# Sparse attention in a two-block transformer: values by pairs of heads in alternating column halves, biases from one reversed row per head

## The chip, the core and the metric

The kernel runs on one core of one Trainium2 chip. Its engines work side by side, each through its own instructions in order: TensorE (PE) multiplies matrices, ScalarE (ACT) and VectorE (DVE) compute on elements, GpSimd (POOL) does a few powers here and issues transfers of its own (the software queue), and SyncE (SP) issues the other transfers (DMA). On-chip memory is SBUF, with 128 partitions, and PSUM, into which PE writes. The metric is the device time of one execution in microseconds (us), as the median of several.

## What is computed

Two blocks of two layers each work on 256 tokens of width 1024 in float32. A layer of block 1 has a large input projection, a retention, a sparse attention (NSA) and a feed-forward part. The change is in the sparse attention, with its 16 heads of 64 columns in 2 groups:

```
def head_bias(dist):
    return jnp.moveaxis(table[t5_bucket(dist)], (-2, -1), (0, 1))
...
lc = jnp.einsum('bghqd,bgnd->bghqn', qx, kc) * scale + head_bias(dc)
pc = masked_softmax(lc, dc >= 0)
oc = jnp.einsum('bghqn,bgnd->bghqd', pc.astype(vc.dtype), vc)
...
ls = jnp.einsum('bghqd,bgqkld->bghqkl', qx, ksel) * scale + sel_bias(ds)
os_ = jnp.einsum('bghqm,bgqmd->bghqd', ps.astype(vsel.dtype), ...)
...
lw = jnp.einsum('bghqd,bgld->bghql', qx, kw) * scale + head_bias(dw)
ow = jnp.einsum('bghql,bgld->bghqd', pw.astype(vw.dtype), vw)
return gx[..., 0:1] * oc + gx[..., 1:2] * os_ + gx[..., 2:3] * ow
```

With 256 tokens every block of keys is selected and the window holds all earlier tokens, so the selected and the window branch both are causal attention over all 256 tokens, with different keys and values. The bias depends on the head and on the distance of query and key alone. The compressed branch has 15 keys.

## The kernel before

PE's foreground is the projections: an item per 512 KB of weights, in a fixed order. SP loads the weights into `raw` (5 buffers; those of the compression into `u`), ACT copies them rounded to `whi`, DVE forms the rest `wlo`, and PE multiplies with both. Everything else (heads of the attention, retention, the set-up of the biases, the end of the compression) is written as generators that run beside the items. A planner at build time (class `Beside`) counts the work of each engine, advances a generator when its step is due by that count and PE has room, and so sets the order on each engine. `use` books an instruction's cost, `arrives` says when a loaded tile is expected, `PACE` (9 us) spaces some steps of the bias set-up. At run time every engine keeps this order and waits on semaphores.

`make_bias` runs once, in layer 1. Two products with a one-hot table give each head's bias by distance: `rb` (16 rows of 384, in DRAM) and `rc` (640 x 16). From `rc` POOL gathers `z<-rc` (L728), and a product with a flip matrix makes `biasc`, the bias of the compressed keys. From `rb` the step `spread` (L711) loads two heads' rows into all 128 partitions (L713, 384 KB) and writes them to `bd`, 128 copies of each head's row in DRAM (L715, 384 KB); eight such pairs cover the 16 heads. A head may start when its rows are there ("bias ready") and the compression has ended (`flags`).

`nsa_head` is one head; four make a quad, two quads share a group. It loads its bias from `bd` with a row step of 383 elements (L873; 4 buffers), so that each partition is shifted by one. PE forms the scores from `KH`, `KL` and the queries; DVE adds the bias and takes the row maxima in one instruction (`add_max`, L203); ACT takes the exponential; the result is scaled and transposed on PE into `PT` (a `z` tile, 6 buffers). Then come the values: four matmuls of `vnat` and `PT` into `O`, a PSUM bank of the quad. Their stationary operand has 64 columns, so a head fills one half of PE's columns: even heads write partitions 0 to 63, odd ones 64 to 127. A matmul of float32 appears in the trace as two records, and each of the trace's weight loads goes with one. After head 3 the quad's compressed part (`vblk`) is added.

Two groups of matmuls of block 2 have the same shape: `b<-z,V` (L1542) does, in one step, a 256 and a 128 wide matmul in one half of the columns and then the same in the other; `b<-w,V` (L1586) does one head, so one half, per step.

Of the kernel before, what the change touches and what calls it, by code (L numbers as in the profile page):

```python
# [10 lines left out]
F32 = mybir.dt.float32  # L11
# [84 lines left out]
SLACK_ROPE, SLACK_STICK, SLACK_DIFF, SLACK_DSA = 2.0, 2.0, 3.0, 2.0  # L96
PUMP_PE = 0.8
BACKLOG = 6.0
PACE = 9.0


@with_exitstack
def tile_kernel(ctx: ExitStack, tc: tile.TileContext, A: dict, out: bass.AP):
    nc = tc.nc
# [8 lines left out]
    dr = ctx.enter_context(tc.tile_pool(name="scratch", bufs=1, space=bass.MemoryType.DRAM))  # L113
# [4 lines left out]
    def zt(shape, dt=F32):  # L118
        return up.tile(shape, dt, name="z", tag="z", bufs=NB_Z)

    def w2(shape, dt=F32):
        return up.tile(shape, dt, name="w", tag="w", bufs=NB_W)
# [4 lines left out]
    def bank(shape):  # L127
        return ps.tile(shape, F32, name="b", tag="b", bufs=8)
# [3 lines left out]
    eng = {"P": 0.0, "A": 0.0, "V": 0.0, "G": 0.0, "D": 0.0}  # L132
    done_at, step, tables, filler = {}, [0.0], [None], [False]
    TABLES = {AF.Exp: 0, AF.Tanh: 0, AF.Gelu_apprx_tanh: 1, AF.Silu: 2, AF.Ln: 3, AF.Sin: 4}

    def key(o):
        return o.tensor.name

    def use(e, ns, outs, ins):
        at = max([done_at.get(key(i), 0.0) for i in ins if hasattr(i, "tensor")] + [0.0])  # L140
        cost = ns / 1e3
        if filler[0]:

            eng[e] += cost
            t = max(eng[e], at + cost)
        else:
            t = eng[e] = max(eng[e], at) + cost
        for o in outs:
            if o is not None:
                done_at[key(o)] = t + 0.1  # L150
        step[0] = max(step[0], t + 0.1)
# [5 lines left out]
    def arrives(t, us):  # L157

        done_at[key(t)] = eng["P"] + us
        step[0] = max(step[0], eng["P"] + us)  # L160

    def width(o):
        n = 1
        for z in o.shape[1:]:
            n *= z
        return n
# [12 lines left out]
    def vec(outs, ins, n=None):  # L179
        use("V", (n or width(outs[0])) / 0.96 + 70, outs, ins)  # L180
# [16 lines left out]
    def copy_v(o, i):  # L197
        nc.vector.tensor_copy(o, i)
        vec([o], [i])
# [12 lines left out]
        nc.vector.reciprocal(o, i)  # L212
        vec([o], [i], 8 * width(o))

    def mm(o, lhsT, rhs, start, stop):
        nc.tensor.matmul(o, lhsT, rhs, start=start, stop=stop, skip_group_check=True)  # L216
        n = width(rhs)
        if rhs.dtype == F32R:
            ns = n / 2.4 * (1 if n >= 256 else 4)
        else:  # L220
            ns = n / 0.6 * width(lhsT) / 128
        use("P", ns, [o], [lhsT, rhs])


    cts = {}
# [5 lines left out]
    def C(name):  # L231
        g, o, n = CW[name]
        return cts[g][:, o:o + n]
# [8 lines left out]
    def warm_up(n):  # L242

        z, b = w2([128, 512]), bank([128, 512])
        nc.vector.memset(z, 0.0)
        for _ in range(n):
            mm(b[:, :256], z[:, :128], z[:, :256], True, True)
# [15 lines left out]
    def split(src, hi, lo, scale=1.0):  # L263
        copy_a(hi, src, scale)
        lo_of(lo, src, hi, scale)
# [174 lines left out]
    S = {}  # L440

    def proj_T(w2d, c0, ncols, x, nkt, evac, r0=0, runs=1, stride=0, pre=None):


        cw = 256 // runs
        for ci, c in enumerate(range(0, ncols, cw)):
            box = {}
            for k0 in range(0, nkt, 4):
                nk = min(4, nkt - k0)

                def fn(pc, ci=ci, k0=k0, nk=nk, box=box):
                    if pre is not None:
                        pre(k0)
                    if k0 == 0:
                        box["b"] = bank([128, 2, 256])
                    hi, lo = pc
                    xx = S[x]
                    for k in range(nk):
                        kk = k0 + k
                        for ct in range(2):  # L460
                            cs = slice(128 * ct, 128 * ct + 128)
                            wh, wl = hi[:, k, cs], lo[:, k, cs]
                            o = box["b"][:, ct, :]
                            mm(o, wh, xx.H(kk), kk == 0 and ct == 0, False)
                            mm(o, wh, xx.L(kk), False, False)
                            mm(o, wl, xx.H(kk), False, kk == nkt - 1)
                    if k0 + nk == nkt:
                        evac(ci, box["b"])

                items.append(Item(fn, spec(w2d, r0 + 128 * k0, nk, c0 + c, cw, runs, stride)))  # L470
# [219 lines left out]
    def make_bias():  # L690
        bp = S["bp"]
        cz = zt([128, 784])
        tab, oneh = cz[:33, 640:656], cz[:33, :640]
        cts[3] = cz[:, 656:784]
        nc.vector.memset(tab, NEG)
        nc.sync.dma_start(tab[:32], A["rel_bias"])
        nc.sync.dma_start(oneh, A["onehot"])
        nc.sync.dma_start(cts[3], A["const_3"])
        flip = C("flip")
        arrives(cz, 6.0)  # L700
        yield
        b = bank([16, 384])
        mm(b, tab, oneh[:, :384], True, True)
        bs = w2([16, 384])
        copy_v(bs, b)

        rb = dr.tile([16, 384], F32, name="rb")
        nc.sync.dma_start(rb, bs)
        S["bd"] = dr.tile([16, 128, 384], F32, name="bd")

        def spread(j):  # L711
            row = zt([128, 2, 384])
            nc.gpsimd.dma_start(row, bass.AP(tensor=rb.tensor, offset=rb.offset + 384 * j,  # L713
                                             ap=[[0, 128], [384, 2], [1, 384]]))
            nc.gpsimd.dma_start(S["bd"][j:j + 2].rearrange("h p k -> p h k"), row)  # L715

        b = bank([128, 5, 16])
        for j in range(5):
            mm(b[:, j, :], oneh[:, 128 * j:128 * j + 128], tab, j == 0, j == 4)
        bs = w2([128, 5, 16])  # L720
        copy_v(bs, b)
        rc = dr.tile([640, 16], F32, name="rc")
        nc.gpsimd.dma_start(rc.rearrange("(j p) h -> p j h", p=128), bs)
        spread(0)

        rv = zt([128, 2, 16, 16])
        for t in range(2):
            nc.gpsimd.dma_start(rv[:, t], bass.AP(tensor=rc.tensor, offset=rc.offset + (159 - 128 * t) * 16,  # L728
                                                  ap=[[16, 128], [256, 16], [1, 16]]))
        spread(2)  # L730
        arrives(rv, 12.0)
        yield
        b = bank([128, 2, 16, 16])
        mm(b, flip, rv, True, True)
        copy_v(S["biasc"], b)
        for j in range(4, 16, 2):
            spread(j)
            S["bias ready"] = j
            step[0] = eng["P"] + PACE
            yield  # L740
        S["bias ready"] = 16

    def block1_layer(i):
        w = A["w_in"][i]
        kvf, flags = {}, set()
# [119 lines left out]

        def nsa_head(qd, hh):
            g, h, Q = qd // 2, 4 * qd + hh, QD[qd]
            while len(flags) < 2 or S.get("bias ready", 0) <= h:
                yield True
            KH, KL, gates, vnat, vblk, biasc = S["KH"], S["KL"], R["gates"], R["vnat"], R["vblk"], S["biasc"]  # L870
            bias = S["bp"].tile([128, 256], F32, name="bias", bufs=4)
            bd = S["bd"]
            nc.gpsimd.dma_start(bias, bass.AP(tensor=bd.tensor, offset=bd.offset + 49152 * h + 127,  # L873
                                              ap=[[383, 128], [1, 256]]))
            arrives(bias, 3.0)
            yield
            Z = zt([128, 800])
# [49 lines left out]
            PT = zt([128, 768])  # L927
            b = bank([128, 2, 2, 128])
# [8 lines left out]
            yield  # L937
            while Q["pv"] != hh:
                yield True
            if hh == 0:  # L940
                Q["O"] = bank([128, 2, 256])
            O = Q["O"]
            e, c = hh % 2, hh // 2
            o = slice(64 * e, 64 * e + 64)
            for br in range(2):
                vs = slice(128 * br + 64 * g, 128 * br + 64 * g + 64)
                mm(O[o, c, :], vnat[:, 0, vs], PT[:, 256 * br:256 * br + 256], c == 0 and br == 0, False)
                mm(O[o, c, 128:], vnat[:, 1, vs], PT[:, 512 + 128 * br:640 + 128 * br], False, False)
            Q["pv"] += 1
            if hh < 3:  # L950
                return
            b = bank([64, 2, 128])
# [5 lines left out]
            for c in range(2):  # L958
                mm(O[:, c, :], vblk[g][:, 2 * c:2 * c + 2, :].rearrange("p a d -> p (a d)"), PcT, False, c == 1)
            k0 = 2 * qd  # L960
            onT = S["onT"]
            split(O, onT.hi[k0 // 4][:, k0 % 4:k0 % 4 + 2, :], onT.lo[k0 // 4][:, k0 % 4:k0 % 4 + 2, :])
            kept["quad", qd] = True
# [38 lines left out]
        def retention(h):  # L1002
# [27 lines left out]
            for n in range(2):  # L1030
                O = bank([128, 512])
                ms = [(0, 128 * n)] + ([(1, 256)] if n else [])
# [816 lines left out]
```

## Time and profile before

| | |
|---|---|
| median of 3 runs | 2214.05 us (2213.95 to 2215.66) |
| the profiled execution | 2216.03 us |
| its span | 2214.3 us |
| PE busy | 2167.8 us, 98% |
| DVE busy | 1486.1 us, 67% |
| ACT busy | 1236.4 us, 56% |
| read from and written to HBM | 376.60 and 4.26 MB |

The span runs from the first to the last instruction of the program; the rest of an execution's time lies around it. Busy is the union of an engine's instructions. Records of PE overlap, and their ends are modelled, so the distance from one start to the next tells more than a duration. PEclk is the share of its clock that PE was granted.

### The profile page before, as it was taken

The numbers are of one execution on the slowest core, as the hardware profiler recorded it, in microseconds if no ns is written. First come the engines' busy times: TensorE is split into PE (matmuls) and PEld (weight loads), VectorE is DVE, ScalarE is ACT, GpSimd is POOL, SyncE is SP. The second block draws the span as 40 slices with busy tenths as digits, with TensorE's granted clock in tenths as the row PEclk, the third lists the DMA queues.
The fourth block names the chain that finished last, engine by engine and source line by source line (L and its number), as shares of the span: only waits on it lengthen the run. The fifth ranks groups of instructions, "written<-read, shape, count | busy, mean of one in ns | idle before, by whom it ended". The sixth has DMA issues, their size and how long they took to land.

```text
span 2214.3 us, 37531 instructions
## 1 busy us (share of the span) xinstructions
PE 2167.8 (98%) x14692; PEld 1973.1 (89%) x14692; DVE 1486.1 (67%) x2773; ACT 1236.4 (56%) x2044; POOL 115.0 (5%) x131
## 2 busy tenths in 40 slices
PE   8899999999999999999999999999999999989998
PEld 7688899899988888998998999988997999988997
DVE  5677765755576777666555887876557888776555
ACT  4466655544455566554444777655445777555443
POOL 2100100000000000000000010100000000100000
PEclk9999999999999999999999999999999999999999
DMA  9854455565676544555655545455655545455553
GB/s 299 281 150 132 141 153 156 176 199 187 194 223 178 150 139 141 146 180 179 185 187 169 175 134 172 139 174 179 190 188 171 165 144 173 147 163 180 190 186 109
DMA packets 299950, 383.31 MB, mean 173 GB/s; under 512 B 16635, under 2 KB 238987, under 8 KB 299772
## 3 DMA queue, kind: packets, MB, share of 16 engines
q1 hardware_dynamic: 296572, 370.12, 54.2%
q0 software_dynamic: 3200, 10.79, 1.5%
q8 instruction: 115, 1.88, 0.3%
q14 instruction: 63, 0.52, 0.1%
HBM read 376.60 MB, written 4.26 MB: 172 GB/s over the span
## 4 chain that ended last, share of the span: by engine, by line
PE 83%; DVE 9%; ACT 3%; DMA 2%; issue 2%; POOL 1%; SPq 0%; POOLq 0%; DVEq 0%; ACTq 0%
PE b L216 80%; DVE wlo L183 3%; PE b L250 3%; DMA raw<-w_in 2%; DVE u L183 2%; ACT z L169 1%; DVE w L183 1%; POOL s L239 1%; ACT u L169 1%; ACT whi L169 1%; DVE z L194 1%; DVE w L194 0%; DVE z L183 0%; ACT L169 0%; DMA w<-a_lambda 0%
## 5 line engine op out<-in xcount | busy, mean ns | idle before, releaser
L183 DVE TENSOR_TENSOR wlo<-raw,whi 128x1024 fp32r<-128x1024 f32 (+1 forms) x670 | 814.7, 1220 | 449.1 <-ACT whi L169 446.8
L169 ACT ACTIVATE whi<-raw 128x1024 fp32r<-128x1024 f32 (+1 forms) x670 | 704.2, 1056 | 656.8 <-PE b L216 464.7
L216 PE MATMUL b<-u,whi 128*128 128x256 f32 x5760 | 1052.8, 285 | 0.0
L216 PEld LDWEIGHTS b<-u,whi 128*128 128x128 f32 x5760 | 902.6, 192 | 10.0 <-issue 5.3
L216 PE MATMUL b<-u,wlo 128*128 128x256 f32 x2880 | 815.9, 283 | 0.0
L216 PE MATMUL b<-whi,u 128*128 128x512 f32 (+2 forms) x2752 | 811.6, 372 | 1.8 <-ACT whi L169 1.6
L216 PEld LDWEIGHTS b<-whi,u 128*128 128x128 f32 x2752 | 502.0, 189 | 90.9 <-issue 4.9
L216 PEld LDWEIGHTS b<-u,wlo 128*128 128x128 f32 x2880 | 552.7, 192 | 0.0
L216 PE MATMUL b<-wlo,u 128*128 128x512 f32 (+2 forms) x1376 | 509.5, 370 | 0.5 <-DVE wlo L183 0.5
L216 PEld LDWEIGHTS b<-wlo,u 128*128 128x128 f32 x1376 | 260.6, 189 | 39.6 <-DVE wlo L183 1.2
L169 ACT ACTIVATE u<-b 64x512 fp32r<-64x512 f32 (+3 forms) x234 | 133.0, 579 | 101.1 <-PE b L250 52.8
L239 POOL TENSOR_TENSOR s<-s,mhalf 128x1 f32<-128x1 f32 (+3 forms) x60 | 77.5, 1292 | 1508.2 <-DVE s L194 1047.1
L169 ACT ACTIVATE z<-z,s 128x256 f32<-128x256 f32 (+2 forms) x304 | 124.5, 425 | 51.6 <-DVE s L203 39.3
L183 DVE TENSOR_TENSOR u<-b,u 128x512 fp32r<-128x512 f32 (+2 forms) x150 | 98.3, 665 | 21.0 <-ACT u L169 16.8
L169 ACT ACTIVATE w<-b 128x512 f32<-128x512 f32 (+3 forms) x150 | 81.1, 547 | 43.2 <-PE b L216 42.0
L250 PE MATMUL b<-const,w 128*128 128x128 f32 (+1 forms) x416 | 65.3, 280 | 19.5 <-DVE w L194 9.3
L250 PEld LDWEIGHTS b<-const,w 128*128 128x128 f32 (+1 forms) x416 | 47.8, 141 | 31.5 <-issue 13.5
L216 PE MATMUL b<-u 128*128 128x256 f32 (+1 forms) x288 | 42.6, 293 | 14.8 <-ACT u L169 8.6
L169 ACT ACTIVATE u<-w 128x512 fp32r<-128x512 f32 x80 | 49.6, 619 | 11.5 <-DVE w L183 11.5
L216 PEld LDWEIGHTS b<-u 128*128 128x128 f32 x288 | 38.2, 196 | 18.5 <-ACT u L169 9.4
L183 DVE TENSOR_TENSOR w<-w 128x512 f32<-128x512 f32 (+3 forms) x94 | 51.9, 566 | 4.0 <-ACT w L169 3.7
L216 PE MATMUL b<-z,vnat 128*64 128x128 f32 (+1 forms) x256 | 46.8, 332 | 0.0
(145 smaller groups left out, 1233.2 us busy)
## 6 DMA issues: line engine op xcount, KB each, us to landing
raw<-w_in SPq DMA_DIRECT2D x268, 512.0 KB, 3.9
raw<-w_ffn_in SPq DMA_DIRECT2D x80, 512.0 KB, 3.6
raw<-w_up SPq DMA_DIRECT2D x64, 512.0 KB, 3.7
raw<-w_down SPq DMA_DIRECT2D x64, 512.0 KB, 3.5
raw<-w_ffn_out SPq DMA_DIRECT2D x44, 512.0 KB, 3.7
raw<-w_o_ret SPq DMA_DIRECT2D x32, 512.0 KB, 3.4
raw<-w_out SPq DMA_DIRECT2D x32, 512.0 KB, 3.8
raw<-w_o_nsa SPq DMA_DIRECT2D x16, 512.0 KB, 3.4
```

Of the source, the lines that this page charges most:

```text
L169: nc.scalar.activation(o, i, func, bias=bias, scale=scale, accum_out=accum_out)
L183: nc.vector.tensor_tensor(out=out, in0=in0, in1=in1, op=op)
L194: nc.vector.scalar_tensor_tensor(out=out, in0=in0, scalar=scalar, in1=in1, op0=op0, op1=op1)
L216: nc.tensor.matmul(o, lhsT, rhs, start=start, stop=stop, skip_group_check=True)
L239: nc.gpsimd.tensor_tensor(o, i, mhalf[:, :n], op=OP.pow)
L250: nc.tensor.transpose(o, i, C("ident")[:i.shape[0], :i.shape[0]])
```

## The change

A head's values are no longer multiplied when it is done: an even head keeps its `PT` and ends, and the odd head that follows does the matmuls of both, eight in a row that go to the two halves of the columns in turn. `mm` has a new argument `share`, by which the planner books each at half its cost. The copies `bd`, and with them `spread` and `PACE`, go. `rb` now holds each row backwards (the copy out of PSUM reads it in reverse), and a head loads its bias from `rb` itself with a row step of one; `add_max` reads the tile backwards. All heads may start once `biasc` is made. The planner expects the gather from `rc` 16 us after its issue, not 12.

```diff
--- before.py
+++ after.py
@@ -96,7 +96,6 @@
 SLACK_ROPE, SLACK_STICK, SLACK_DIFF, SLACK_DSA = 2.0, 2.0, 3.0, 2.0
 PUMP_PE = 0.8
 BACKLOG = 6.0
-PACE = 9.0
 
 
 @with_exitstack
@@ -212,14 +211,14 @@
         nc.vector.reciprocal(o, i)
         vec([o], [i], 8 * width(o))
 
-    def mm(o, lhsT, rhs, start, stop):
+    def mm(o, lhsT, rhs, start, stop, share=1.0):
         nc.tensor.matmul(o, lhsT, rhs, start=start, stop=stop, skip_group_check=True)
         n = width(rhs)
         if rhs.dtype == F32R:
             ns = n / 2.4 * (1 if n >= 256 else 4)
         else:
             ns = n / 0.6 * width(lhsT) / 128
-        use("P", ns, [o], [lhsT, rhs])
+        use("P", ns * share, [o], [lhsT, rhs])
 
 
     cts = {}
@@ -701,19 +700,11 @@
         yield
         b = bank([16, 384])
         mm(b, tab, oneh[:, :384], True, True)
+
         bs = w2([16, 384])
-        copy_v(bs, b)
-
-        rb = dr.tile([16, 384], F32, name="rb")
+        copy_v(bs, b[:, ::-1])
+        rb = S["rb"] = dr.tile([16, 384], F32, name="rb")
         nc.sync.dma_start(rb, bs)
-        S["bd"] = dr.tile([16, 128, 384], F32, name="bd")
-
-        def spread(j):
-            row = zt([128, 2, 384])
-            nc.gpsimd.dma_start(row, bass.AP(tensor=rb.tensor, offset=rb.offset + 384 * j,
-                                             ap=[[0, 128], [384, 2], [1, 384]]))
-            nc.gpsimd.dma_start(S["bd"][j:j + 2].rearrange("h p k -> p h k"), row)
-
         b = bank([128, 5, 16])
         for j in range(5):
             mm(b[:, j, :], oneh[:, 128 * j:128 * j + 128], tab, j == 0, j == 4)
@@ -721,24 +712,17 @@
         copy_v(bs, b)
         rc = dr.tile([640, 16], F32, name="rc")
         nc.gpsimd.dma_start(rc.rearrange("(j p) h -> p j h", p=128), bs)
-        spread(0)
 
         rv = zt([128, 2, 16, 16])
         for t in range(2):
             nc.gpsimd.dma_start(rv[:, t], bass.AP(tensor=rc.tensor, offset=rc.offset + (159 - 128 * t) * 16,
                                                   ap=[[16, 128], [256, 16], [1, 16]]))
-        spread(2)
-        arrives(rv, 12.0)
+        arrives(rv, 16.0)
         yield
         b = bank([128, 2, 16, 16])
         mm(b, flip, rv, True, True)
         copy_v(S["biasc"], b)
-        for j in range(4, 16, 2):
-            spread(j)
-            S["bias ready"] = j
-            step[0] = eng["P"] + PACE
-            yield
-        S["bias ready"] = 16
+        S["bias ready"] = True
 
     def block1_layer(i):
         w = A["w_in"][i]
@@ -865,13 +849,14 @@
 
         def nsa_head(qd, hh):
             g, h, Q = qd // 2, 4 * qd + hh, QD[qd]
-            while len(flags) < 2 or S.get("bias ready", 0) <= h:
+            while len(flags) < 2 or "bias ready" not in S:
                 yield True
             KH, KL, gates, vnat, vblk, biasc = S["KH"], S["KL"], R["gates"], R["vnat"], R["vblk"], S["biasc"]
             bias = S["bp"].tile([128, 256], F32, name="bias", bufs=4)
-            bd = S["bd"]
-            nc.gpsimd.dma_start(bias, bass.AP(tensor=bd.tensor, offset=bd.offset + 49152 * h + 127,
-                                              ap=[[383, 128], [1, 256]]))
+            rb = S["rb"]
+            nc.gpsimd.dma_start(bias, bass.AP(tensor=rb.tensor, offset=rb.offset + 384 * h + 1,
+                                              ap=[[1, 128], [1, 256]]))
+            bias = bias[:, ::-1]
             arrives(bias, 3.0)
             yield
             Z = zt([128, 800])
@@ -937,16 +922,21 @@
             yield
             while Q["pv"] != hh:
                 yield True
-            if hh == 0:
+            Q["pv"] += 1
+            if hh % 2 == 0:
+                Q["PT"] = PT
+                return
+
+            if hh == 1:
                 Q["O"] = bank([128, 2, 256])
-            O = Q["O"]
-            e, c = hh % 2, hh // 2
-            o = slice(64 * e, 64 * e + 64)
+            O, c = Q["O"], hh // 2
+            pair = [(slice(0, 64), Q.pop("PT")), (slice(64, 128), PT)]
             for br in range(2):
                 vs = slice(128 * br + 64 * g, 128 * br + 64 * g + 64)
-                mm(O[o, c, :], vnat[:, 0, vs], PT[:, 256 * br:256 * br + 256], c == 0 and br == 0, False)
-                mm(O[o, c, 128:], vnat[:, 1, vs], PT[:, 512 + 128 * br:640 + 128 * br], False, False)
-            Q["pv"] += 1
+                for o, P in pair:
+                    mm(O[o, c, :], vnat[:, 0, vs], P[:, 256 * br:256 * br + 256], c == 0 and br == 0, False, 0.5)
+                for o, P in pair:
+                    mm(O[o, c, 128:], vnat[:, 1, vs], P[:, 512 + 128 * br:640 + 128 * br], False, False, 0.5)
             if hh < 3:
                 return
             b = bank([64, 2, 128])
```

On PE, in layer 1, the first head of the first quad before (`kh0`, `kl0` are its keys, `z_1345` its `PT`, `b_1399` the quad's `O`, `whi`/`wlo` weights of the foreground, `u` activations):

```order
L216 MATMUL b_1383<-kh0_166,u_553 128x272
L216 MATMUL b_1383<-kl0_168,u_553 128x272
L216 MATMUL b_1386<-kh0_166,u_553 128x256
L216 MATMUL b_1386<-kl0_168,u_553 128x256
L216 MATMUL b_1399<-z_1345,vnat_171 64x256
L216 MATMUL b_1399<-z_1345,vnat_171 64x128
L216 MATMUL b_1399<-z_1345,vnat_171 64x256
L216 MATMUL b_1399<-z_1345,vnat_171 64x128
L216 MATMUL b_1410<-whi_1327,u_92 128x512
```

and the first pair of the same quad now (`z_1358` and `z_1413` are the `PT` of heads 0 and 1, `b_1462` is `O`):

```order
L215 MATMUL b_1406<-whi_1369,u_93 128x512
L215 MATMUL b_1462<-z_1358,vnat_171 64x256
L215 MATMUL b_1462<-z_1413,vnat_171 64x256
L215 MATMUL b_1462<-z_1358,vnat_171 64x128
L215 MATMUL b_1462<-z_1413,vnat_171 64x128
L215 MATMUL b_1462<-z_1358,vnat_171 64x256
L215 MATMUL b_1462<-z_1413,vnat_171 64x256
L215 MATMUL b_1462<-z_1358,vnat_171 64x128
L215 MATMUL b_1462<-z_1413,vnat_171 64x128
L215 MATMUL b_1399<-whi_1393,u_94 128x512
```

What was four matmuls of one head is eight of two, in turn; the weights around them keep their order.

On POOL, from the set-up of the biases to the first head's load, before (the row of `z` to `bd` comes six more times):

```order
L723 DMA rc_269<-w_267 128x5x16
L713 DMA z_271<-rb_258 128x768
L728 DMA z_274<-rc_269 128x16x16 x2
L713 DMA z_277<-rb_258 128x768
L715 DMA bd_260<-z_271 128x2x384
L713 DMA z_430<-rb_258 128x768
L715 DMA bd_260<-z_277 128x2x384
```

and now:

```order
L714 DMA rc_268<-w_266 128x5x16
L718 DMA z_270<-rc_268 128x16x16 x2
L857 DMA bias_1084<-rb_258 128x256
L857 DMA bias_1086<-rb_258 128x256
L857 DMA bias_1436<-rb_258 128x256
L857 DMA bias_1471<-rb_258 128x256
L1033 TENSOR_SCALAR s_855<-s_855 128x1
```

The sixteen transfers between `rb`, `z` and `bd` are gone, and the first four heads' loads follow the gather from `rc`.

On PE, the product with the flip matrix before (`z_274` is the gather, `z_194` holds the matrix, `b_402` collects a tile of the projection by keys and values):

```order
L216 MATMUL b_402<-u_92,wlo_288 128x256
L216 MATMUL b_427<-z_274,z_194 128x512
L216 MATMUL b_402<-u_94,whi_346 128x256
L216 MATMUL b_402<-u_95,whi_346 128x256
L216 MATMUL b_402<-u_94,wlo_347 128x256
```

and now:

```order
L215 MATMUL b_478<-u_92,wlo_390 128x256
L215 MATMUL b_503<-z_270,z_194 128x512
L215 MATMUL b_514<-u_312,w_369 32x256 x4
L215 MATMUL b_478<-u_94,whi_422 128x256
L215 MATMUL b_478<-u_95,whi_422 128x256
```

It stands 48 rows of PE's order later, in the next tile of the projection and right ahead of the first matmuls of the compression.

## Rows read from the trace of the kernel before

**Rows 1.** The page's first part: busy us (share of the span) x instructions.

```profile
PE 2167.8 (98%) x14692; PEld 1973.1 (89%) x14692; DVE 1486.1 (67%) x2773; ACT 1236.4 (56%) x2044; POOL 115.0 (5%) x131
```

**Rows 2.** Stretches of layers 1 and 2: length, engines' busy us (records), PEclk, DMA share, GB/s.

```profile
30.20:85.40 55.20, 46.67 (x331) 40.97 (x330) 35.95 (x59) 25.70 (x35) 14.17 (x21) 0.91 1.06 362
629.70:672.10 42.40, 42.40 (x331) 38.26 (x333) 31.64 (x55) 20.93 (x30) 0.00 (x0) 1.00 0.82 258
85.40:190.20 104.80, 104.80 (x674) 90.50 (x673) 76.29 (x199) 62.60 (x123) 6.42 (x12) 1.00 0.52 152
672.10:776.70 104.60, 104.60 (x673) 90.24 (x672) 75.32 (x199) 62.29 (x125) 5.45 (x12) 1.00 0.53 155
```

**Rows 3.** PE's waits from 28 to 86 us: total us, times, longest.

```profile
PE b L216 <- ACT u L169: 7.5, 1, 7.5
PE b L216 <- DMA z<-rc: 0.8, 1, 0.8
```

**Rows 4.** The chain of waits from 30 to 90 us: start, us, what.

```profile
35.24 17.92 DMA raw<-w_in
...
57.74 12.82 DMA raw<-w_in
```

**Rows 5.** DMA from 28 to 86 us: queue and share; issues, KB each, us to landing.

```profile
q0 software_dynamic: 1856, 7.12, 33.6%
...
raw<-w_in SPq DMA_DIRECT2D x17, 512.0 KB, 11.4
bd<-z POOLq DMA_DIRECT2D x8, 384.0 KB, 6.8
z<-rb POOLq DMA_DIRECT2D x7, 384.0 KB, 7.9
```

**Rows 6.** DMA from 86 to 376 us: issues.

```profile
raw<-w_in SPq DMA_DIRECT2D x53, 512.0 KB, 3.7
```

**Rows 7.** The stretch after PE's wait, with columns as in Rows 2.

```profile
77.30:83.70 6.40, 6.12 (x22) 5.34 (x23) 3.42 (x6) 3.44 (x5) 0.00 (x0) 0.50 1.09 350
```

**Rows 8.** Timeline of PE around one head's values: start us, us, instruction.

```profile
138.12 0.28 PE L216 MATMUL b<-kh,u 128*128 128x256 f32 x1
138.23 0.28 PE L216 MATMUL b<-kl,u 128*128 128x256 f32 x1
138.44 1.51 PE L216 MATMUL b<-z,vnat 128*64 128x256 f32 x8
139.88 0.50 PE L216 MATMUL b<-whi,u 128*128 128x512 f32 x1
```

**Rows 9.** Stretches of the attention, instructions of `vnat` alone: PE and PEld busy, ACT.

```profile
138.00:376.00 238.00, 23.42 (x128) 15.03 (x128) 0.00 (x0) 1.00 0.50 147
728.00:963.00 235.00, 23.43 (x128) 15.03 (x128) 0.00 (x0) 1.00 0.49 144
```

**Rows 10.** Timeline of PE where two heads' values stand together.

```profile
290.65 2.22 PE L216 MATMUL b<-z,vnat 128*64 128x256 f32 x16
```

**Rows 11.** Timeline of PE in block 2: two halves in one step.

```profile
1275.55 0.88 PE L216 MATMUL b<-z,V 128*64 128x256 f32 x8
```

**Rows 12.** Timeline of PE in block 2: one half in one step.

```profile
1868.94 0.86 PE L216 MATMUL b<-w,V 128*64 128x256 f32 x4
```

**Rows 13.** Groups of DVE by shape: count, busy us, mean ns, idle before.

```profile
L203 DVE CUSTOM_DVE_ANT_0 z<-b,bias 128x128 f32<-128x128 f32 x128 | 34.5, 285 | 18.0 <-PE b L216 17.6
...
L183 DVE TENSOR_TENSOR w<-b,posT 64x120 f32<-64x120 f32 x32 | 7.6, 276 | 2.1 <-PE b L216 1.9
```

**Rows 14.** The bias tiles: who waited for the loads (nobody), and us to landing.

```profile
who waited for it (us, times):
...
DMA to landing us min/median/max: 2.3/2.8/6.7
```

## Prediction

> **What bounds the kernel now.** I read the page's busy shares first: TensorE (PE) is busy for 98% of the span [rows 1], so a term counts only if it shortens PE's own work or removes one of its few idle stretches. Block 1 runs the same code twice, once per layer, and only layer 1 also sets up the biases. The table of stretches therefore gives layer 1 a twin [rows 2]: from the position transposes to the last product of the compression's key half, layer 1 takes 55.2 us and layer 2 42.4 us, and from there to the end of the first quad of heads 104.8 and 104.6 us. All that the two layers differ in is the 12.8 us of the first stretch. The waits of PE in that stretch name 7.5 us for ACT `u` and 0.8 us for `z<-rc`, the gather that the bias set-up makes [rows 3]. The chain of waits goes past ACT: it holds two loads of w_in, issued at 35.24 and 57.74, that took 17.9 and 12.8 us [rows 4]. A load of the same 512 KB takes 3.7 us once the set-up is over [rows 6]. In the set-up all loads share the DMA engines with eight `z<-rb` and eight `bd<-z` transfers of 384 KB, and the software queue that carries them holds 33.6% of the 16 engines [rows 5]; the stretch moves 362 GB/s at a share of 1.06 [rows 2]. So the copies of the bias rows delay the weights, ACT waits for them in its own order, and the key split of head 0 that PE needs stands behind them. After the 7.5 us of idleness PE is granted 0.50 of its clock until 83.7 [rows 7], which costs half of those 6.4 us, 3.2 us. Idle time and slow clock are 11.5 of the 12.8 us.
>
> **The values of the heads.** Each head is four matmuls, eight records, all in one half of the columns. The timeline shows such a group: it starts at 138.44, the next matmul starts at 139.88, so 1.44 us; the printed 1.51 us ends 0.07 after that next start [rows 8]. The table by tile holds 128 records and 23.42 us in each layer [rows 9]. There are 30 such stretches, 28 of one head and two where two heads happened to stand together; taking 0.07 off each of the 30, 46.85 - 2.1 = 44.7 us for both layers.
> After the change eight matmuls of two heads stand together and change halves at each step. Block 2 has the nearest rows: `b<-w,V` is four records (a 256 and a 128 wide matmul) in one half and takes 0.86 us [rows 12]; `b<-z,V` is the same four in one half and four more in the other, and takes 0.88 [rows 11]. The second half costs 0.02 us. So I take 1.44 + 0.02 = 1.46 us for a pair, and 16 x 1.46 = 23.4 us for both layers: 21.3 us less. Entering a group costs as well: 0.21 us from the matmul before it, where 0.11 us is usual between full-width ones [rows 8]. 14 entries fewer are 1.4 us. Together **22.7 us**; PE is never idle around these groups, so all of it is on the path. Bounds: the second half free gives 23.0. The other end is the two adjacent heads in the order as written, 2.22 - 0.07 = 2.15 us [rows 10]: 44.7 - 34.4 + 1.4 = 11.7. I stay by 1.46, since the 0.88 is of halves that belong together, as in the change, while in the 2.15 us the second head's matmuls stand behind all of the first's.
> How far PE can look past its order is what the two rows differ in. If it started matmuls strictly in the written order, each when its own half is free, the `b<-z,V` group (256 and 128 of one half, then of the other) would start its last record 0.55 us later than one half alone: 0.86 + 0.55 = 1.41 us, where the row has 0.88 [rows 11, 12]. The Trainium skill, page "TensorE: Matmul & The Clock Gate", section "The mechanism", says that matmuls start and end strictly first in, first out. The row of block 2 disagrees: 0.88, not 1.41. What that rule would make of the sum is among the rivals.
>
> **The bias rows.** Six things change.
> First, the sixteen transfers of 384 KB go, 6.3 MB. The stretch moves 55.2 us x 362 GB/s = 20.0 MB [rows 2]; without them 13.7 MB. If layer 1 then ran like layer 2, 12.8 us would go, but its product with `flip`, which layer 2 lacks, stays: 1024 columns at the 0.94 ns of a PV record's column (1.44 us for 1536) are 1.0 us, so 11.8 us at most, with the `z<-rc` wait in it. Against the full 11.8 speaks that 13.7 MB in 43.4 us are 316 GB/s, more than the 258 of layer 2 [rows 2], which had loaded ahead. At the 362 of the full queue they need 38 us, so the queue fits, with little to spare, and I leave 1.3 us for a wait that remains: **10.5 us**, with 6 and 11.8 as bounds.
> Second, the `flip` product stands one item later in PE's order. That moves, and doesn't lengthen, its work, and the wait of 0.8 us for `z<-rc` is covered by that item.
> Third, POOL has no copies left between its gather and the bias loads, and SP's order stays the same. POOL isn't on the chain.
> Fourth, each head reads its 128 x 256 bias from one row of `rb`, at the same 128 KB. Before, nobody waited for these loads, which land after 2.3 to 6.7 us [rows 14], because four buffers let them start about four heads ahead. Cost nothing; if they took 20 us, that lead (heads come some 16 us apart) would still hide them.
> Fifth, the bias is read backwards by VectorE, 6 instructions per head, 192 in all. No row shows a negative step. The nearest is a strided read, 64 x 120 out of PSUM in 276 ns, against 285 ns for the 128-wide sum with the bias [rows 13]; by it, the cost is 0. A doubling would add 192 x 0.13 = 25 us of VectorE work, which is busy for 76.3 of 104.8 us there [rows 2], so it would hide. The Trainium skill, page "Vector Engine (DVE) Microarchitecture Reference", section "Performance modes — why throughput varies by op and dtype", counts an operand with a negative step among what was not measured, so the page decides nothing.
> Sixth, an even head keeps its transposed values until its partner is done, and the order shows each pair's matmuls before the next pair needs that buffer: no wait added. PACE goes with the copies it spaced; the heads start at the same matmul of the weights as before.
>
> **The sum.** The profiled execution took 2216.0 us, of which the span is 2214.3. 2216.0 - 22.7 - 10.5 = 2182.8. The median of the runs, 2214.05, lies 2.0 below the profiled one, so **2181 us** for a median, 1.5% less.
>
> **The rivals.**
> *The start stays bound by the weights.* The 13.7 MB could come in the wrong places: the small rows of the first 30 us leave the queue behind, and head 0's key still stands behind a late split. Against it: without the copies the queue has 38 us of work for 43. If 9 of the 12 us remain, the gain is 22.7 + 3: 2188.
> *Strict order on PE.* In the changed order a record then starts when the one before has started and its own half is free: with 0.22 us for a 256-wide record and 0.11 for a 128-wide, the pair's last record starts at 1.51 us, a single head's at 1.21. A pair is 1.74 us, the sum 16 x 0.28 = 4.5 worse: 2185.5. This is the rule of the TensorE page above; block 2's row speaks against it.
> *The halves don't overlap at all*, since two heads' operands and a second wait come in between: a pair is 2.88 us, only the start's 10.5 remains: 2203.5. Both of rows 10 and 11 speak against it.
> *Reading backwards is slow, and VectorE becomes the bound.* This is the way to a slower kernel. VectorE is free for 28.5 of 104.8 us [rows 2], in which about five heads' sums are done, 30 instructions: each may take 0.95 us more before VectorE is full. It eats all of the 33 us gain (16.5 per layer, 96 instructions, 0.17 us each) only at 0.95 + 0.17 us more, some 1.4 us per instruction, five times the row's 285 ns. At ten times, 2.85 us, the loss is 96 x (2.57 - 0.95) = 155 us a layer: about 2490. Nothing in the rows points to it.
>
> **How the numbers follow.** Forecast 0.78; start stays bound 0.10; strict order 0.05; no overlap 0.03; slow reading 0.02; something else, as a new stall of the planner's order, 0.02. Range: the best ends, 23.0 + 11.8, give 2179; I go 3 us further for small stalls in the two layers that the new order may lose. The upper end takes in the start's 6 (2185.5) and reaches to the bound start (2188) with 2 us for new waits: **2176 to 2190**. Faster by over 0.2%, which is 4.4 us and about what a measurement of this kernel can tell from no change: 0.95; within it 0.02; slower 0.03.
>
> **What would show it.** In the changed kernel: 16 groups of 16 records of `b<-z,vnat`, about 1.46 us each and some 24.5 us in all by the same table; no 7.5 us wait for ACT `u`, no 0.50 of the clock near 80 us; the first stretch at about 45 us and the weights' loads in it near 5 us; sums with the bias still at 285 ns. Wrong are: groups of 1.7 us or more (order), a first stretch above 49 us (weights), sums with the bias over 400 ns, or an idle PE between 85 and 376 us.

## The result, and the profile after

The change took 2180.19 us (median of 4, 2179.47 to 2181.69), the kernel before 2214.86 beside it: a ratio of 0.9843, interval 0.9826 to 0.9860, so 34.7 us less. The forecast was 2181, the range 2176 to 2190. The profiled execution after took 2179.47 us, with a span of 2177.5.

The same table of stretches as in [rows 2], now of the changed kernel (from the position transposes to the fifth product of the compression in layers 1 and 2, and from there to the end of the first quad; columns as there):

```profile
28.70:72.00 43.30, 43.30 (x333) 38.53 (x334) 35.79 (x59) 24.94 (x34) 4.49 (x6) 1.00 1.01 312
604.20:646.60 42.40, 42.40 (x327) 38.25 (x326) 31.72 (x55) 20.95 (x30) 0.00 (x0) 1.00 0.84 265
72.00:170.70 98.70, 98.70 (x662) 86.28 (x661) 73.55 (x195) 61.84 (x126) 5.57 (x12) 1.00 0.55 159
646.60:745.50 98.90, 98.90 (x662) 86.33 (x661) 73.57 (x195) 61.77 (x126) 5.57 (x12) 1.00 0.55 159
```

Layer 1's first stretch fell from 55.2 to 43.3 us, within 0.9 of its twin, and that is the product with `flip`, which only layer 1 has (0.95 us, below). PE is busy for all of it and its clock is granted in full, where [rows 2] had 0.91. The list of PE's waits from 28 to 380 us is empty, where [rows 3] had 7.5 and 0.8 us. The chain of waits from 28 to 75 us, half made of loads before [rows 4], is now PE alone:

```profile
by line: PE b L215 99.9%; PE b L249 0.5%
```

The DMA view of 28 to 72 us, as [rows 5]:

```profile
q0 software_dynamic: 304, 0.80, 7.9%
...
raw<-w_in SPq DMA_DIRECT2D x17, 512.0 KB, 6.0
...
bias<-rb POOLq DMA_DIRECT2D x4, 128.0 KB, 6.3
```

A load of weights lands after 6.0 us, not 11.4. The DMA engines are still full (a share of 1.01 at 312 GB/s), but the weights come in time.

The values, in the table by tile (as [rows 9]) and in PE's timeline around the first pair (as [rows 8]):

```profile
120.00:360.00 240.00, 12.17 (x128) 7.93 (x128) 0.00 (x0) 1.00 0.54 155
700.00:930.00 230.00, 12.17 (x128) 7.92 (x128) 0.00 (x0) 1.00 0.53 153
```

```profile
131.73 0.39 PE L215 MATMUL b<-whi,u 128*128 128x512 f32 x1
132.04 1.52 PE L215 MATMUL b<-z,vnat 128*64 128x256 f32 x16
133.50 0.50 PE L215 MATMUL b<-whi,u 128*128 128x512 f32 x1
133.83 0.40 PE L215 MATMUL b<-wlo,u 128*128 128x512 f32 x1
```

The same 128 records a layer take 12.17 us where they took 23.42, in eight groups of two heads. A group runs from 132.04 to 133.50, 1.45 us when the starts are taken to the nanosecond, and a single head took 1.44 [rows 8].

To see where the time goes along the program I set the two profiled executions side by side by the start of the same matmul of the weights (k counts the records with `whi` or `wlo` ahead of it; their order on PE is the same in both kernels):

```
k weight matmuls on     before    after   difference   what lies before it
     24                   24.5     23.0      -1.5      loads of the start; the edit isn't reached
    264                   60.4     58.0      -2.4      the product with flip
    324                   86.4     73.0     -13.4      where PE waited before
    456                  114.8    101.3     -13.5      start of the heads, layer 1
   1824                  376.6    351.3     -25.3      end of the heads, layer 1
   3600                  645.0    619.6     -25.4
   5256                  963.2    926.1     -37.1      end of the heads, layer 2
  12767                 2208.5   2171.8     -36.7      end
```

So 12.0 us come from the start (13.5 less the 1.5 ahead of the edit), 11.8 from the heads of layer 1 and 11.7 from those of layer 2.

### The profile page after: what moved, and what is told of

The parts are those of the page before. It is cut to its first block, busy times and chain, and to the rows that moved or that the text cites. A ratio compares the mean times of both kernels' runs of the same rounds, so it can differ in the third digit from the quotient of the medians.

```text
span 2177.5 us, 37501 instructions
## 1 busy us (share of the span) xinstructions
PE 2141.6 (98%) x14692; PEld 1957.6 (90%) x14692; DVE 1487.4 (68%) x2773; ACT 1234.8 (57%) x2044; POOL 99.5 (5%) x115
## 4 chain that ended last, share of the span: by engine, by line
PE 84%; DVE 8%; ACT 4%; issue 2%; POOL 1%; DMA 1%; SPq 0%; POOLq 0%; DVEq 0%; ACTq 0%
PE b L215 82%; DVE wlo L182 3%; PE b L249 3%; DVE u L182 1%; ACT z L168 1%; ACT u L168 1%; POOL s L238 1%; DVE w L182 1%; ACT whi L168 1%; DVE z L193 0%; DVE w L193 0%; ACT L168 0%; DVE z L182 0%; DVE s L207 0%; DVE z L1390 0%
## 5 line engine op out<-in xcount | busy, mean ns | idle before, releaser
L238 POOL TENSOR_TENSOR s<-s,mhalf 128x1 f32<-128x1 f32 (+3 forms) x60 | 72.1, 1202 | 1511.4 <-DVE s L193 1049.9
L168 ACT ACTIVATE w<-x 128x512 f32<-128x512 f32 x44 | 27.4, 625 | 33.6 <-DVE x L182 30.6
```

Source lines behind the costliest of these rows:

```text
L168: nc.scalar.activation(o, i, func, bias=bias, scale=scale, accum_out=accum_out)
L238: nc.gpsimd.tensor_tensor(o, i, mhalf[:, :n], op=OP.pow)
```

## The experiments

The theory: two gains that add up. The halves of PE's columns work at the same time because the order alternates, and the start loses its wait because the weights no longer share the DMA engines with the copies. Against it stand the rivals of the prediction, and two more: that it is enough to put two heads together, and that the heads' wait for their own rows, or the place of the second set-up step, made the start slow. Each result is beside runs of the kernel before on the same chip.

**Pairs, but not alternating.** One edit to the change:

```diff
-            for br in range(2):
-                vs = slice(128 * br + 64 * g, 128 * br + 64 * g + 64)
-                for o, P in pair:
-                    mm(O[o, c, :], ...)
-                for o, P in pair:
-                    mm(O[o, c, 128:], ...)
+            for o, P in pair:
+                for br in range(2):
+                    vs = slice(128 * br + 64 * g, 128 * br + 64 * g + 64)
+                    mm(O[o, c, :], ...)
+                    mm(O[o, c, 128:], ...)
```

> The change with one edit: the eight matmuls of a pair still stand together, but the first head's four come before the second's four. Theory (the halves must alternate within what PE can look ahead): a group takes 2.15 us as the two adjacent heads of the kernel before did, not 1.45, so 16 x 0.70 = 11.2 us more than the change: 2191 us. Rival (putting two heads together is what pays, by fewer entries and by an overlap that any order gives): 2180 us, groups of 1.45 us.

Measured: 2192.41 us (2191.68 to 2192.93) against 2215.63 before, a ratio of 0.9894 (0.9877 to 0.9910). PE's timeline at the first pair:

```profile
134.01 2.22 PE L215 MATMUL b<-z,vnat 128*64 128x256 f32 x16
136.16 0.50 PE L215 MATMUL b<-whi,u 128*128 128x512 f32 x1
```

From 134.01 to 136.16 the pair takes 2.15 us, as the two neighbours of [rows 10] did. 16 x 0.70 = 11.2 is the whole of the loss: along the weight matmuls this execution loses 11.2 us on that of the change from the start of the heads in layer 1 to their end in layer 2. So an order in which one head comes after the other doesn't give the overlap of the turn. Standing together pays by itself as well: 44.7 us of groups became 34.4, and this version is 11.7 us faster than the change without its value part (2204.14, below).

**The turn taken every second matmul.**

```diff
                 for o, P in pair:
                     mm(O[o, c, :], ...)
-                for o, P in pair:
                     mm(O[o, c, 128:], ...)
```

> The change, but the halves change after every two matmuls (a head's 256 and 128 wide of one branch, then the partner's), as block 2's b<-z,V does, not after every one. Theory (PE looks a few records past a blocked one, four here): groups of 1.45 us, 2180 us. Rival (matmuls start in strict order, each when its own half is free): a group is 0.2 us or more longer, 2183.5 us or more.

Measured: 2180.67 us (2179.21 to 2181.96); the change itself took 2181.74 beside it. The group:

```profile
133.03 1.57 PE L215 MATMUL b<-z,vnat 128*64 128x256 f32 x16
134.53 0.50 PE L215 MATMUL b<-whi,u 128*128 128x512 f32 x1
```

1.50 us, 0.05 more than in full alternation, which is 0.8 us for 16 pairs and not to be seen in the medians. Under strict order the second half could not begin before both matmuls of the first had started, some 0.55 us after it. In the trace two 256 wide records start 0.014 us apart at the head of the group. That rival is out.

**The bias part alone.** The change with each head multiplying its values by itself, as before:

```diff
-            Q["pv"] += 1
-            if hh % 2 == 0:
-                Q["PT"] = PT
-                return
-            if hh == 1:
+            if hh == 0:
                 Q["O"] = bank([128, 2, 256])
...
+            for br in range(2):
+                mm(O[o, c, :], vnat[:, 0, vs], PT[:, 256 * br:256 * br + 256], c == 0 and br == 0, False)
+                mm(O[o, c, 128:], vnat[:, 1, vs], PT[:, 512 + 128 * br:640 + 128 * br], False, False)
+            Q["pv"] += 1
```

> The change without its value part: each head multiplies its values alone, as before; biases from the one reversed row, no copies. Theory (two separate gains that add up): the start's 12 us alone, 2215 - 12 = 2203 us, with 30 groups or so of 1.44 us of values. Rival (the start's gain needs the shorter values, or the pairs' order in the planner): 2214 us.

Measured: 2204.14 us (2203.34 to 2204.74) against 2215.63, a ratio of 0.9948 (0.9933 to 0.9962): 11.5 us. PE has no wait from 28 to 90 us.

**The value part alone.** The kernel before with the other half of the diff (the lines on `pair`, `Q["PT"]` and `share`, none on the biases).

> The kernel before with the value part of the change alone: pairs in alternating halves, the copies of the bias rows as before. Theory: 23.5 us less than before by the values, 2215 - 23.5 = 2191 us, and the 7.5 us wait of PE near 70 us stays. Rival (part of the 23.5 us in the two attention stretches comes from the lighter transfers): 2195 us or more.

Measured: 2191.84 us (2190.50 to 2195.81), a ratio of 0.9895 (0.9881 to 0.9910): 23.8 us. PE's waits from 28 to 90 us are those of before again, 7.2 us for the two of [rows 3], which had 8.3 (the third, 0.3 us, is in the trace of before too):

```profile
PE b L216 <- ACT u L169: 5.9, 1, 5.9
PE b L216 <- DMA z<-rc: 1.3, 1, 1.3
PE b L216 <- DVE u L183: 0.3, 1, 0.3
```

11.5 + 23.8 = 35.3 us against 34.7 for both together: the parts add up.

**The copies made and not read.** The change with the old copies at their old places; the heads read `rb`, and none waits for the copies:

```diff
         nc.gpsimd.dma_start(rc.rearrange("(j p) h -> p j h", p=128), bs)
+        spread(0)
...
+        spread(2)
         arrives(rv, 16.0)
...
         S["bias ready"] = True
+        for j in range(4, 16, 2):
+            spread(j)
+            step[0] = eng["P"] + 9.0
+            yield
```

> The change, but the eight loads of rows into 128 partitions and the eight copies to DRAM are still made, at the places of before; no head reads them, and all heads may start at once. Theory (the copies' traffic delays the weights): the wait returns, some 12 us more than the change: 2192 us, weights landing after 11 us in the first stretch. Rival (what counted was that heads waited for their rows, or the place of the second step): 2180 us, since nothing waits for the copies here.

Measured: 2194.60 us (2192.92 to 2195.53), a ratio of 0.9904 (0.9889 to 0.9919). PE's wait is back, the weights land late again, and the chain of waits holds two loads of them as in [rows 4] (PE's waits from 28 to 90 us; DMA from 28 to 84; the chain from 30 to 90):

```profile
PE b L215 <- ACT u L168: 7.3, 1, 7.3
PE b L215 <- DVE u L182: 0.3, 1, 0.3
```

```profile
q0 software_dynamic: 1654, 6.32, 31.2%
...
raw<-w_in SPq DMA_DIRECT2D x17, 512.0 KB, 11.5
bd<-z POOLq DMA_DIRECT2D x7, 384.0 KB, 7.6
```

```profile
35.24 15.65 DMA raw<-w_in
...
55.48 13.15 DMA raw<-w_in
```

Nothing reads these copies, so it is their traffic that holds up the weights. Along the weight matmuls this execution loses 10.1 us on that of the change between k = 264 and k = 324, where PE waits. That is less than the start's 12.0, so the traffic alone isn't all of it: the 1.0 us before k = 264, with the wait for `z<-rc`, doesn't come back, as the second step stands later here, and 0.9 is open. The medians differ by 12.9 us, 2194.60 from the change's 2181.74 on another chip, where I expected 12. The rest of that lies mostly behind the heads, where two executions of the change itself differ by over 1 us as well.

**The second step as early as before.**

```diff
-        arrives(rv, 16.0)
+        arrives(rv, 12.0)
```

> The change with the second set-up step expected 12 us after the gather's issue, as before, not 16: the product with the flip matrix stands 48 rows earlier in PE's order. Theory (the later step only covers a wait of about 1 us): the gather landed at 37.9 us in the changed kernel and this place of PE's order is reached at 38 to 39, so no wait or one below 1 us: 2180 to 2181 us. Rival (the later step carries a good part of the start's 12 us): 2184 us or more, with a wait for the gather of some us.

Measured: 2181.18 us (2179.77 to 2182.56), beside 2181.74 for the change. The product with `flip` stands at 38.43 and follows the matmul before it without a wait:

```profile
38.16 0.28 PE L215 MATMUL b<-u,wlo 128*128 128x256 f32 x1
38.43 1.10 PE L215 MATMUL b<-z 128*128 128x512 f32 x2
38.97 0.80 PE L215 MATMUL b<-u,whi 128*128 128x256 f32 x2
```

The later step brings nothing once the copies are gone: the gather comes in time at either place. With the copies it does, since the run before this one has no wait for `z<-rc`. So either edit takes away the 0.8 us of [rows 3].

**The change again, and pairs in block 2 too.** The groups of block 2 that did one head at a time, made in the same way:

```diff
             yield from in_turn(("c", ch), hh)
+            turn["c", ch] = hh + 1
+            if hh % 2 == 0:
+                outs["pt", ch] = pt
+                return
...
+            for e, o, hs, P in pair:
+                mm(O[o, c, :], V["cv"][:, 0, hs], P[:, :256], c == 0, False, 0.5)
+            for e, o, hs, P in pair:
+                mm(O[o, c, 128:], V["cv"][:, 1, hs], P[:, 256:], False, c == 1, 0.5)
```

> The change itself once more, to see how far its first 13 us, which the edit doesn't touch, and block 2 differ from run to run: 2180 us, with 1 us either way.

> The change, and the same pairing for the heads of block 2 that do their values alone (b<-w,V, 64 records that took 8.5 us in nine groups). Theory: eight pairs of 0.65 us with their exits make about 6 us, so 2 to 3 us less where PE is the bound: 2178 us. Rival (that part of block 2 waits for other engines or for a pair's later head, so the time is taken up elsewhere): 2180 us or more, with PE idle there.

Measured: the change 2181.74 us (2181.06 to 2182.75), 1.7 above the 2180 expected, where I had allowed 1, and with the pairs in block 2 2176.85 (2176.74 to 2176.98), a ratio to before of 0.9822 (0.9809 to 0.9836). Every execution of this version is faster than every one of the change. PE's groups by shape, of the change and then of this version (count, busy us, mean ns):

```profile
L215 PE MATMUL b<-w,V 128*64 128x256 f32 x32 | 7.1, 401 | 0.0
...
L215 PE MATMUL b<-w,V 128*64 128x128 f32 x32 | 4.3, 273 | 0.0
```

```profile
L215 PE MATMUL b<-w,V 128*64 128x256 f32 x32 | 5.1, 398 | 0.0
...
L215 PE MATMUL b<-w,V 128*64 128x128 f32 x32 | 3.1, 272 | 0.0
```

By tile, from first start to the next other matmul, the groups fell from 8.5 us in nine stretches to 6.1 in six. Along the weight matmuls of the two profiled executions, the stretches around these groups (k = 7200 to 8000 and 10300 to 11000) gained 1.9 and 1.1 us; another 1.3 us lie elsewhere. Two executions of the change itself differ by 0.1 us or less in these two stretches, but by 1.3 over block 2. So about 3 us are the edit's, the upper end of what was expected, and where the rest of the 4.9 between the medians comes from stays open.

## Why the prediction was right

**What bounds the kernel** was read rightly: PE, and in the first stretch the weights behind the copies. The twin stretch of layer 2 was the best row of all. It gave 12.8 us as all that could be had, 11.8 of them without the product with `flip`, and 11.9 came (55.2 less 43.3).

**The values** were put at 22.7 us; the traces have 23.5 in the two layers, and the part alone 23.8. The pair of 1.46 us is 1.45, so the groups went from 44.7 to 23.2 us, 21.5 and not 21.3. The remaining 2.0 us are 14 groups fewer to enter and to leave. Entering costs what I took it for, 0.09 to 0.10 us in all groups of both kernels but two, so 1.4 us. The sum left out a second cost, behind the group: where a full-width record of 256 columns or more follows, the one after it comes 0.10 us later than usual (133.50 to 133.83 in the timeline above, where 0.23 is usual). Before, 18 groups had such a record behind them, now 6. With these 1.3 us it would be more than the 2.0, so some of it comes back elsewhere; where, stays open. The upper bound on a group, 2.15 us by [rows 10], is the experiment without alternation: it measured that number. Taking the value near [rows 11] was right: that row, too, has two halves in reach of each other, as the turn every second matmul shows.

**The start** is the term that was mis-sized: 10.5 us forecast, 12.0 by the traces and 11.5 by the part alone. I left 1.3 us for a wait that would remain, since 13.7 MB in 43.4 us would ask for 316 GB/s. The stretch did move 312 GB/s at a share of 1.01, but PE didn't wait at all, though the loads of weights landed after 6.0 us, not the 5 I named as a sign. The product with `flip` was put at 1.0 us, and takes 0.95 (PE, after, to the next matmul):

```profile
43.44 1.02 PE L215 MATMUL b<-z 128*128 128x512 f32 x2
44.39 0.64 PE L215 MATMUL b<-u,w 128*32 128x256 f32 x8
```

So the upper bound of 11.8 was right, and what came lies at it.

**The edits put at nothing.** The sums with the bias, read backwards, take what they took, 285 ns, as [rows 13] (groups of DVE, after):

```profile
L202 DVE CUSTOM_DVE_ANT_0 z<-b,bias 128x128 f32<-128x128 f32 x128 | 34.4, 285 | 13.4 <-PE b L215 13.1
```

So the way to a slower kernel was closed: the negative step cost this instruction nothing. The bias loads from `rb` land a little later than those from `bd`, but nobody waits for them (bias tiles, after, against 2.3/2.8/6.7 in [rows 14]):

```profile
who waited for it (us, times):
...
DMA to landing us min/median/max: 3.1/3.5/6.6
```

The `flip` product's later place hid no wait, as its run shows. The empty list of PE's waits in the attention, from 28 to 380 us and from 600 to 960 in layer 2, says the same of the transposed values that even heads keep.

**The sum.** 33.2 us forecast, 34.7 by the medians and 36.7 in the table of the two profiled executions, of which 1.5 lie ahead of the edit. Those 1.5 us are no effect: in the ten profiled executions of this study, whose kernels are the same up to there, the weight matmul at k = 24 began between 23.0 and 25.0 us. Both terms came out a little above their best ends (23.5 by the traces against 23.0, 12.0 against 11.8), 2.3 us more than forecast. That the median is only 0.8 off is in part luck: the forecast counts from 2214.05, and the kernel before took 2214.86 beside the change.

**The rivals.** The bound start (2188) is out by the 43.3 us stretch; strict order (2185.5) by the run with the turn every second matmul, and by its own mark, groups of 1.7 us; no overlap (2203.5) by 1.45 us per pair; slow reading by the 285 ns.

## What to carry to other kernels

Where PE is the bound, look for matmuls whose stationary operand fills half the columns, and set them in pairs that write different halves, in turn; the order within the pair was worth as much here as the pairing, 11 of 23 us. A copy that only prepares data has a price on the DMA engines where the weights are late: look at how long the same load takes with and without it. And where a program runs the same code twice, the second run is the bound for the first, less what only the first does.

## What the runs showed that I had not expected

PE's reach past its order can be read from three orders of the same sixteen records: in turn 1.45 us, the turn every second matmul 1.50, one head after the other 2.15. The trace of the last shows where the second head comes in. PE's records of `vnat` in its first group, from 134.00 on (length, busy us and records, PEclk, DMA share, GB/s):

```profile
134.00:134.70 0.70, 0.69 (x4) 1.00 0.78 269
134.00:134.72 0.72, 0.71 (x6) 1.00 0.81 282
```

Four records start before 134.70, and then two at once, at 134.710 and 134.716, though in one half a 256 wide record takes 0.22 us before the next. The seventh and eighth to start are 256 wide as well, where the written order has two of 128 there. So records of the second head start ahead of earlier ones of the first, the ninth with the fifth: a reach of four records. The turn every second matmul fits it: there the record written fifth starts with the first. It was not tried with other shapes.

Full DMA engines are no sign by themselves. At a share of 1.01 and 312 GB/s PE lost nothing. With the unread copies the same stretch (columns as in [rows 2]) lasts 10.0 us longer:

```profile
29.41:82.75 53.34, 45.77 (x333) 40.29 (x334) 36.07 (x59) 25.44 (x35) 12.93 (x19) 0.94 1.04 359
```

The shares, 1.01 and 1.04, hardly tell the two apart; the times to landing, 6.0 and 11.5 us, do. How much of the 6.3 MB the engines would have borne was not tried.
